# Spreading the preparation of attention groups evenly over the tiles of the group before, with a third PSUM bank for late maxima

## The chip, the cores and the metric

The kernel runs on one core of a Trainium2 chip. The time is device microseconds of one execution. TensorE (PE) multiplies matrices into PSUM, VectorE (DVE) and ScalarE (ACT) read PSUM, GpSimd (POOL) works on SBUF alone, and SyncE (SP) issues most of the DMAs. PSUM has eight banks of 128 x 512 fp32, and the kernel gives each a role.

## The reference, cut to what matters

The model is two layers over 1024 latent tokens with a prefix of 256 context tokens, width 1024, all in fp32. Layer 0 has global grouped attention (A, 8 heads on 2 key heads, with normed and rotated queries and keys) and windowed attention (B, 8 heads on 2 key heads, band of +-128 tokens, the whole context and a learned sink logit). Layer 1 has a convolution module and a neighbourhood attention with 8 heads and a bias table. The part at stake is the softmax of all of these:

```
def gqa_attend(q, k, v, bias=None, sink=None):
    s = jnp.einsum("bqhgd,bkhd->bhgqk", q, k, preferred_element_type=jnp.float32) * ATTN_SCALE
    if bias is not None:
        s = s + bias
    if sink is not None:
        ...
    else:
        p = jax.nn.softmax(s, axis=-1)
    return jnp.einsum("bhgqk,bkhd->bqhgd", p.astype(v.dtype), v)
```

The softmax needs the largest score of each query row. The kernel computes it ahead of the attention itself.

## The kernel before, in words

**Precision.** Every operand is split into a high part (rounded to fp32r) and a low part, so a product is three matmuls (`mm3`, lines 332 to 334), or for scores two (lines 509 and 513) and for the values three (460 to 462). `split` (lines 312 and 315) makes the two parts: a copy on ACT, a subtraction on POOL or DVE.

**Groups and tiles.** Attention runs in groups. In layer 0 a group is one block of 128 queries of four heads that share a key head, so 512 columns; there are four units (key heads, order `ORDER`: two of B, two of A) of ten query blocks each, in the order `QORD`. A group's tiles are blocks of 128 keys: two for a block of context queries, four or five for a block of B, ten for a block of A. In layer 1 a group is one head and one half of the columns, with seven tiles; there are 16. `attn_gen` (line 477) walks through all tiles: score products into one of two banks `st`, exponential on ACT (line 521), `split`, and three tiles later (`look`) the products with the values into the bank `ov` (`flush`). After the last tile of a group DVE turns the sums round, takes the reciprocal and scales the output (lines 470 to 473 and `finish`, 670 to 672).

**Preparation.** What a group needs before its first tile is made by two generators whose steps are handed out between the tiles of earlier groups. `attn_prep` (line 402) loads the queries (layer 0, line 607) or the bias rows (layer 1, line 1279), lets four (layer 1: eight) empty steps pass, then goes through `maxes`: a score product into a bank `mx` (lines 620, 632, 640; layer 1: 1312, 1320), and a reduction on DVE (622, 633, 641; 1314, 1321), with a step after each; then one reduction over the pieces (416 to 426, with the sink where there is one). A preparation has 2 maxima for a context block, 6 for a block of B, 10 for a block of A, 6 for a group of layer 1. `attn_fin` (line 430) lets two empty steps pass, transposes the maxima on PE into another `mx` bank (437), and DVE multiplies them with a mask into the extra rows of `QL` (438). The second score product (513) brings them in, so it must wait for 438.

During group g the steps of `attn_fin` of group g + 1 are handed out first, then those of `attn_prep` of group g + 2. How many come with each tile is a whole number that the kernel works out for each group:

```
g.step = -(-(18 * len(ids) + 4) // len(g.tiles))
```

Half of it (rounded down) comes after the tile's score products, the rest after the flush; at the group's last tile all that is left is handed out. It is 3 for ten tiles, 5 for five, 11 for two, and 4 for the seven of layer 1.

**Fill.** `weave` mixes other work in between the tiles: in layer 0 the projections of the next unit and the output products (lines 332 to 334), in layer 1 its own projections and output products. At the end of a unit a stretch is left without fill.

**Order.** The program text only gives each instruction a priority (its place, shifted for fill by `FL`). A planner simulates the engines and puts on each engine's queue what is ready, the oldest first. Tiles that share a tag share buffers in turn: `mx` has two banks, `tr` has one. `tr` serves the transposition of new queries and keys (line 879), the modulation (184, 189) and the sums of the norms (259).

Of the kernel before, what the change touches and what calls it, by code (L numbers as in the profile page):

```python
# [55 lines left out]
FIN = (2, 2)  # L56
# [20 lines left out]
ORDER = (2, 3, 0, 1)  # L77
# [11 lines left out]
def tile_kernel(ctx: ExitStack, tc: tile.TileContext, a, out):  # L89
# [14 lines left out]
    def bank(tag, name):  # L104
        if tag == "pp" and solo[0]:
            turn[0] += 1
            tag = ("pp", "mx")[turn[0] // 2 % 2]
        return ps.tile([P, 512], F32, tag=tag, name=name, bufs=BUFS[tag])

    uid = [0]  # L110
# [332 lines left out]
    def attn_gen(pool, groups, vshare, look, nexts=None):  # L443
# [4 lines left out]
        cnt = [0]  # L448

        def flush():  # L450
            g, t, ph, pl = pend.pop(0)
# [33 lines left out]
        if layer[0]:  # L485
            groups[0].copy()
        for gi, g in enumerate(groups):
            ids = [gi + 2] if gi + 2 < len(groups) else []
            if nexts is not None and gi in nexts:
                ids = nexts[gi]  # L490
            nx = [preps[k] for k in ids]
            if gi + 1 < len(groups):
                nx.insert(1 if ids[:1] == [gi + 1] else 0, attn_fin(groups[gi + 1]))
            g.next = chain.from_iterable(nx)
            g.step = -(-(18 * len(ids) + 4) // len(g.tiles))
        for g, t in items[:AHEAD]:
            g.ahead(t)
        for x, (g, t) in enumerate(items):
# [26 lines left out]
            if t == len(g.tiles) // 2:  # L525
                g.gate()
            for _ in range(g.step // 2):
                next(g.next, None)
            yield
            if len(pend) > look:  # L530
                flush()
            for _ in range(g.step - g.step // 2):
                next(g.next, None)
            if t == len(g.tiles) - 1:
                for _ in g.next:
                    pass
# [64 lines left out]
    def group0(u, qb):  # L601
        isb = u >= 2
# [11 lines left out]
        def maxes(QH, mp):  # L614
            KA = KAs[u]
            for i2 in range(2):
                mx = bank("mx", nm("mx"))
                for i in range(2):
                    hd = 2 * i2 + i
                    PE.matmul(mx[:, i * 256 : (i + 1) * 256], QH[:, hd * P : (hd + 1) * P], KA[:, 0:256],  # L620
                              start=True, stop=True)
                VE.tensor_reduce(mp[:, 2 * i2 : 2 * i2 + 2, 0], mx.rearrange("p (i k) -> p i k", i=2),
                                 axis=AX.X, op=ALU.max)
                yield
            if qb < 2:
                return
            for hd in range(4):
                q = QH[:, hd * P : (hd + 1) * P]
                if not isb:
                    for k in range(2):  # L630
                        mx = bank("mx", nm("mx"))
                        PE.matmul(mx, q, KA[:, 256 + k * 512 : 768 + k * 512], start=True, stop=True)  # L632
                        VE.tensor_reduce(mp[:, hd, 1 + k : 2 + k], mx, axis=AX.X, op=ALU.max)  # L633
                        yield
                else:
                    lo, hi = max(qb - 1, 2), min(qb + 2, 10)
                    n = (hi - lo) * P
                    mo = (lo - (qb - 1)) * P
                    mx = bank("mx", nm("mx"))
                    PE.matmul(mx[:, :n], q, KA[:, lo * P : hi * P], start=True, stop=True)  # L640
# [25 lines left out]
        def finish(ov, rb):  # L666
# [9 lines left out]
            else:  # L676
# [7 lines left out]
                  tiles=[(k, 0, 512, x) for k, x in kt], den=den, finish=finish)  # L684
        g.prep = attn_prep(kvp, g)
        return g

# [332 lines left out]
    with ExitStack() as l1x:  # L1020
# [241 lines left out]
        def group1(gi, hd, hf):  # L1262
# [41 lines left out]
            def maxes(QH, mp):  # L1304
                KA = Ks[hd % len(Ks)][0]
                for b in (1, 2, 0, 3):
                    if b in (1, 0):
                        mx = bank("mx", nm("mx1"))
                        b0 = 1 - b
# [8 lines left out]
                    n, o = (r1 - r0) * NW, 256 + hf * 640 + r0 * NW  # L1318
                    mx = bank("mx", nm("mx1"))
                    PE.matmul(mx[:, :n], QH[:, b * P : (b + 1) * P], KA[:, o : o + n], start=True, stop=True)  # L1320
# [12 lines left out]
            def finish(ov, rb):  # L1333
# [6 lines left out]
                if i == 3:  # L1340
# [4 lines left out]
                      k=lambda: Ks[hd % len(Ks)], load_v=None, v=lambda k: Vs[gi % 2][:, k if k < 2 else k - 5 * hf, :])  # L1345
            g.prep = attn_prep(kvs[-1], g)
            return g

# [266 lines left out]
```

## Time and profile before

| | |
|---|---|
| median of 3 runs | 1559.18 us (1557.75 to 1565.87) |
| profiled execution | 1559.91 us |
| its span, first to last instruction | 1558.1 us |
| instructions | 21469 |
| mean granted PE clock | 0.965 |
| maxima's products in layer 0 | 160 (line 620), 128 (632), 64 (640) |
| maxima's products in layer 1 | 64 (1312), 64 (1320) |

A row of an engine gives its busy time, a row of waits the engine and line that waited, what it waited for, the sum of the waits in us, their number and the longest. A row of a timeline gives the start and the length in us, the engine, line, operation, tiles and shape, and in brackets how long the engine was idle before. Windowed groups run from about 130 to 489 us, the two units of global attention to about 890, layer 1's attention from about 1205 to 1500.

### The profile page before, as it was taken

The numbers are of one execution on the slowest core, as the hardware profiler recorded it, in microseconds if no ns is written. First come the engines' busy times: TensorE is split into PE (matmuls) and PEld (weight loads), VectorE is DVE, ScalarE is ACT, GpSimd is POOL, SyncE is SP. The second block draws the span as 40 slices with busy tenths as digits, with TensorE's granted clock in tenths as the row PEclk, the third lists the DMA queues.
The fourth block names the chain that finished last, engine by engine and source line by source line (L and its number), as shares of the span: only waits on it lengthen the run. The fifth ranks groups of instructions, "written<-read, shape, count | busy, mean of one in ns | idle before, by whom it ended". The sixth has DMA issues, their size and how long they took to land.

```text
span 1558.1 us, 21469 instructions
## 1 busy us (share of the span) xinstructions
PE 1459.1 (94%) x7084; PEld 1175.6 (75%) x7084; DVE 1050.0 (67%) x2113; ACT 746.9 (48%) x1418; POOL 801.5 (51%) x637
## 2 busy tenths in 40 slices
PE   6899999998998989999999878999999899989995
PEld 2786978896896768876866657888887688868875
DVE  2833557579579765466677846999756566577866
ACT  3721434444435564447556663443334355455563
POOL 3530434455445765557656664665632344364675
PEclk9899999999999999999999889999999899999996
DMA  9473315422312245121112012111445777878632
GB/s 366 161 244 124 108 57 181 143 70 92 119 51 79 92 151 177 54 68 50 51 31 92 7 34 86 58 55 41 142 159 192 216 204 236 263 227 243 183 111 108
DMA packets 154168, 199.83 MB, mean 128 GB/s; under 512 B 14716, under 2 KB 95816, under 8 KB 154056
## 3 DMA queue, kind: packets, MB, share of 16 engines
q1 hardware_dynamic: 147392, 186.88, 38.0%
q10 hardware_dynamic: 6664, 11.57, 2.3%
q8 instruction: 56, 0.92, 0.2%
q14 instruction: 56, 0.46, 0.1%
HBM read 148.07 MB, written 49.02 MB: 126 GB/s over the span
## 4 chain that ended last, share of the span: by engine, by line
PE 79%; DVE 13%; DMA 3%; issue 2%; ACT 2%; POOL 1%; SPq 0%; DVEq 0%; POOLq 0%; ACTq 0%
PE p L332 7%; PE p L333 7%; PE p L334 7%; PE ov L460 4%; PE ov L462 4%; PE ov L461 4%; PE st L509 4%; PE st L513 4%; PE po L333 4%; PE po L332 4%; PE po L334 4%; PE pq L332 3%; PE pq L334 3%; PE pq L333 3%; PE pm L184 2%
## 5 line engine op out<-in xcount | busy, mean ns | idle before, releaser
L315 POOL TENSOR_TENSOR pl<-pf,ph 128x512 fp32r<-128x512 f32 (+4 forms) x321 | 396.8, 1247 | 375.8 <-ACT ph L312 328.7
L521 ACT ACTIVATE pf<-st 128x512 f32<-128x512 f32 x284 | 166.3, 597 | 210.3 <-PE st L513 171.0
L315 POOL TENSOR_TENSOR wl<-wr,wh 128x512 fp32r<-128x512 f32 (+2 forms) x131 | 170.5, 1313 | 141.4 <-ACT wh L312 121.4
L312 ACT CAST ph<-pf 128x512 fp32r<-128x512 f32 (+4 forms) x364 | 209.2, 588 | 29.0 <-PE ov L461 16.7
L332 PE MATMUL p<-hh,wh 128*128 128x512 f32 x448 | 178.2, 398 | 5.3 <-ACT hh L312 2.8
L333 PE MATMUL p<-hl,wh 128*128 128x512 f32 x448 | 176.1, 394 | 0.6 <-POOL hl L315 0.6
L334 PE MATMUL p<-hh,wl 128*128 128x512 f32 x448 | 173.7, 394 | 0.0
L509 PE MATMUL st<-QH,KAt 128*128 128x512 f32 (+4 forms) x364 | 140.9, 388 | 8.9 <-ACT pf L521 8.1
L460 PE MATMUL ov<-ph,Vt 128*128 128x512 f32 (+4 forms) x364 | 142.5, 392 | 5.6 <-DVE y L670 4.3
L462 PE MATMUL ov<-pl,Vt 128*128 128x512 f32 (+4 forms) x364 | 141.9, 390 | 1.8 <-POOL pl L315 1.8
L461 PE MATMUL ov<-ph,Vt 128*64 128x512 f32 (+4 forms) x364 | 140.5, 386 | 0.0
L513 PE MATMUL st<-QL,KBt 68*128 68x512 f32 (+4 forms) x364 | 136.4, 386 | 2.0 <-DVE QL L438 2.0
L1085 DVE SCALAR_TENSOR_TENSOR cps<-U,taps,cps 128x512 f32<-128x512 f32 x184 | 126.4, 751 | 0.9
L312 ACT CAST wh<-wr 128x512 fp32r<-128x512 f32 (+2 forms) x134 | 81.2, 613 | 92.3 <-DMA wr<-in_od_d_dram 19.1
L332 PEld LDWEIGHTS p<-hh,wh 128*128 128x128 f32 x448 | 85.1, 190 | 23.8 <-ACT hh L312 3.0
L333 PEld LDWEIGHTS p<-hl,wh 128*128 128x128 f32 x448 | 85.2, 190 | 18.7 <-POOL hl L315 1.7
L334 PEld LDWEIGHTS p<-hh,wl 128*128 128x128 f32 x448 | 85.1, 190 | 17.5
L633 DVE TENSOR_REDUCE mp<-mx 128x1 f32<-128x512 f32 x128 | 85.2, 681 | 17.4 <-PE mx L632 16.5
L332 PE MATMUL pq<-wh,hh 128*128 128x384 f32 x256 | 88.4, 345 | 2.8 <-ACT hh L312 2.8
L509 PEld LDWEIGHTS st<-QH,KAt 128*128 128x128 f32 x364 | 69.7, 192 | 26.5 <-ACT pf L521 11.9
L954 DVE SCALAR_TENSOR_TENSOR x<-po,modT,x 128x512 f32<-128x512 f32 (+1 forms) x72 | 47.0, 657 | 62.1 <-PE po L334 61.7
L333 PE MATMUL pq<-wl,hh 128*128 128x384 f32 x256 | 87.4, 342 | 0.0
(280 smaller groups left out, 3470.8 us busy)
## 6 DMA issues: line engine op xcount, KB each, us to landing
mw<-in_mod_w_dram SPq DMA_DIRECT2D x16, 1024.0 KB, 5.5
Q<-qs SPq DMA_DIRECT2D x40, 256.0 KB, 2.2
QH<-Q SPq DMA_DIRECT2D x80, 128.0 KB, 2.7
mw<-in_mod_w_dram SPq DMA_DIRECT2D x16, 512.0 KB, 6.7
wr<-in_od_d_dram SPq DMA_DIRECT2D x32, 256.0 KB, 3.2
wr<-in_ev_qkv_dram SPq DMA_DIRECT2D x16, 384.0 KB, 5.2
KAt<-KD SPq DMA_DIRECT2D x16, 384.0 KB, 5.9
wr<-in_od_wo_dram SPq DMA_DIRECT2D x22, 256.0 KB, 3.3
```

The lines of the kernel that those rows point to most:

```text
L312: acts.append(SC.copy(hi, src))
L315: (GP if leng == "g" else VE).tensor_tensor(lo, src, hi.bitcast(F32), op=ALU.subtract)
L332: PE.matmul(o, lh, rh, start=first, stop=False)
L333: PE.matmul(o, lh, rl, start=False, stop=False)
L334: PE.matmul(o, ll, rh, start=False, stop=last)
L460: PE.matmul(o, V[:, 64:192], ph[:, :n], start=(t == 0), stop=False)
L461: PE.matmul(g.ov[0:64, q0 : q0 + n], V[:, 0:64], ph[:, :n], start=False, stop=False)
L462: PE.matmul(o, V[:, 64:192], pl[:, :n], start=False, stop=(last and g.sink is None))
L509: sts.append(PE.matmul(st[:, :n], KA[:, cs], g.QH[:, q0 : q0 + n], start=True, stop=False))
L513: PE.matmul(st[:, :n], KB[0:68, cs], g.QL[0:68, q0 : q0 + n], start=False, stop=True)
L521: acts.append(SC.activation(pf[:, :n], st[:, :n], AF.Exp, scale=1.0 if g.bias else SCALE))
L1085: VE.scalar_tensor_tensor(pc, uc, w, pc, op0=ALU.mult, op1=ALU.add)
```

## The change

A group now carries `units`, the number of steps of its preparation, and `done`, how many steps it has handed out. `advance` hands out steps until `pace` times the number of half tiles so far is reached; `pace` is the number of steps that belong to the group divided by its half tiles, no longer rounded up. In layer 0 a group of two tiles gets a pace of 2.5 a half tile, so ten steps; what is left goes, ahead of its own, to the next group, whose pace counts them in. Everywhere else what is left at the last tile is still handed out there. `mbank` gives every third maximum the bank `tr` in place of `mx`: for all of layer 1, and in layer 0 for the last unit's query blocks from the fourth of `QORD` on. Nothing is added to or taken from the computation.

```
+    third = [0]
+    def mbank(name, wide):
+        third[0] += wide
+        return bank("tr" if wide and third[0] % 3 == 0 else "mx", name)
...
+        def advance(g, n):
+            while g.done < g.pace * n:
+                g.done += 1
+                next(g.next, None)
...
+        rest, over = [], 0
         for gi, g in enumerate(groups):
...
             nx = [preps[k] for k in ids]
             if gi + 1 < len(groups):
                 nx.insert(1 if ids[:1] == [gi + 1] else 0, attn_fin(groups[gi + 1]))
-            g.next = chain.from_iterable(nx)
-            g.step = -(-(18 * len(ids) + 4) // len(g.tiles))
+            units = sum(groups[k].units for k in ids) + FIN[layer[0]] + 1 + over
+            g.spill = not layer[0] and len(g.tiles) == 2 and gi + 1 < len(groups)
+            g.next = chain.from_iterable(rest + nx)
+            rest, over, g.pace = [], 0, units / len(g.tiles) / 2
+            if g.spill:
+                g.pace = 2.5
+                rest, over = [g.next], units - 10
...
-            for _ in range(g.step // 2):
-                next(g.next, None)
+            advance(g, 2 * t + 1)
             yield
             if len(pend) > look:
                 flush()
-            for _ in range(g.step - g.step // 2):
-                next(g.next, None)
-            if t == len(g.tiles) - 1:
+            advance(g, 2 * t + 2)
+            if t == len(g.tiles) - 1 and not g.spill:
                 for _ in g.next:
                     pass
             yield
...
         def maxes(QH, mp):
             KA = KAs[u]
+            wide = u == ORDER[-1] and QORD.index(qb) > 2
             for i2 in range(2):
-                mx = bank("mx", nm("mx"))
+                mx = mbank(nm("mx"), wide)
...
+        g.units, g.done = 4 + 2 + (0 if qb < 2 else 4 if isb else 8) + 1, 0
...
-                        mx = bank("mx", nm("mx1"))
+                        mx = mbank(nm("mx1"), True)
...
+            g.units, g.done = 15, 0
```

More of the change, by code (lines that the diff above doesn't have):

```diff
@@ L630, in maxes @@
                     for k in range(2):
-                        mx = bank("mx", nm("mx"))
+                        mx = mbank(nm("mx"), wide)
                         PE.matmul(mx, q, KA[:, 256 + k * 512 : 768 + k * 512], start=True, stop=True)
@@ L638, in maxes @@
                     mo = (lo - (qb - 1)) * P
-                    mx = bank("mx", nm("mx"))
+                    mx = mbank(nm("mx"), wide)
                     PE.matmul(mx[:, :n], q, KA[:, lo * P : hi * P], start=True, stop=True)
@@ L1318, in maxes @@
                     n, o = (r1 - r0) * NW, 256 + hf * 640 + r0 * NW
-                    mx = bank("mx", nm("mx1"))
+                    mx = mbank(nm("mx1"), True)
                     PE.matmul(mx[:, :n], QH[:, b * P : (b + 1) * P], KA[:, o : o + n], start=True, stop=True)
```

## The prediction

> **What bounds the kernel now.** I read the page's busy table and clock row first, then the chain that ended last, then what TensorE (PE) waited for, then the stretches of the two attention stages, and at the end the instructions around three of the waits.
>
> ```profile
> span 1558.1 us, 21469 instructions
> PE 1459.1 (94%) x7084; PEld 1175.6 (75%) x7084; DVE 1050.0 (67%) x2113; ACT 746.9 (48%) x1418; POOL 801.5 (51%) x637
> PEclk9899999999999999999999889999999899999996
> ...
> PE 79%; DVE 13%; DMA 3%; issue 2%; ACT 2%; POOL 1%; SPq 0%; DVEq 0%; POOLq 0%; ACTq 0%
> ```
>
> PE is the bound: 94% busy, 79% of the chain, and the change adds and removes no instruction. So all that can be won is PE's idle time (1558.1 - 1459.1 = 99.0 us) and the time at a lowered clock. Where that idle time lies is in the next view (columns: stretch, its length, then busy us of each engine, then the granted clock):
>
> ```profile
> 130.00:489.00 359.00, 348.39 (x1827) 291.88 (x1827) 240.86 (x578) 146.48 (x311) 161.99 (x120) 1.00 0.31 101
> 489.00:727.00 238.00, 228.45 (x1081) 181.38 (x1080) 151.94 (x270) 128.20 (x232) 148.34 (x111) 0.99 0.32 101
> 727.00:890.00 163.00, 152.67 (x683) 115.83 (x681) 122.84 (x219) 98.78 (x175) 101.03 (x78) 0.96 0.16 48
> 1205.00:1500.00 295.00, 280.65 (x1392) 231.90 (x1392) 197.71 (x461) 149.58 (x297) 138.84 (x126) 0.96 0.76 222
> ```
>
> The windowed groups (130 to 489), the first global unit (to 727), the last unit (to 890) and layer 1's attention (1205 to 1500) hold 10.6 + 9.6 + 10.3 + 14.3 = 44.8 us of idle PE; the other 54 us lie in the start, the middle and the tail, which the change doesn't touch. In the last unit DVE is busy 122.84 of 163.00 us, its highest share of the four. Of the 44.8 us, these waits of PE belong to the preparation steps (us in total, times, longest):
>
> ```profile
> PE mx L632 <- DVE mp L633: 7.6, 14, 2.1
> PE mx L1320 <- DVE mp L1321: 4.1, 3, 3.4
> PE mx L1312 <- DMA KAt<-KD: 3.5, 1, 3.5
> PE trn L437 <- DVE nmt L426: 2.1, 3, 1.3
> PE mx L620 <- DVE QL L438: 2.1, 3, 1.1
> PE st L513 <- DVE QL L438: 2.0, 1, 2.0
> PE mx L640 <- DVE mp L622: 1.6, 2, 0.9
> PE mx L1320 <- DVE mp L1314: 1.4, 3, 0.8
> PE trn L437 <- DVE nmt L416: 1.0, 1, 1.0
> PE mx L632 <- DVE mp L622: 0.4, 2, 0.2
> ```
>
> Three kinds: a product for a maximum waits until DVE has emptied one of the two banks (layer 0: 7.6 + 1.6 + 0.4 = 9.6; layer 1: 4.1 + 1.4 = 5.5); the transposition of the finished maxima (L437), or the product behind it in the same banks (L620), waits for DVE (2.1 + 1.0 + 2.1 = 5.2); and a maximum of layer 1 came before its keys had landed (3.5).
>
> **A stall costs twice.** These rows are the stretches just behind five such stalls:
>
> ```profile
> 583.42 0.50 PE L632 MATMUL mx<-KAt,QH 128*128 128x512 f32 x1 [2.06 <-DVE mp L633]
> 800.94 0.27 PE L437 MATMUL trn<-ident,nmt 128*4 128x128 f32 x1 [1.04 <-DVE nmt L416]
> 802.60 0.50 PE L620 MATMUL mx<-KAt,QH 128*128 128x256 f32 x2 [1.09 <-DVE QL L438]
> ...
> 523.64:527.05 3.41, 3.33 (x10) 2.67 (x11) 3.41 (x7) 2.42 (x6) 1.45 (x1) 0.50 0.54 181
> 585.08:588.49 3.41, 3.41 (x12) 2.63 (x11) 1.12 (x3) 0.60 (x1) 1.30 (x2) 0.50 1.05 364
> 803.54:806.95 3.41, 3.29 (x9) 2.08 (x8) 2.98 (x6) 2.31 (x5) 1.85 (x2) 0.50 0.05 15
> 1370.15:1373.56 3.41, 3.41 (x12) 2.81 (x11) 1.33 (x5) 1.54 (x4) 2.13 (x3) 0.50 1.10 366
> 1380.39:1383.80 3.41, 3.41 (x9) 2.25 (x9) 3.30 (x9) 0.83 (x3) 3.37 (x3) 0.50 0.83 254
> ```
>
> After 1.04 + 1.09 us of idle PE the granted clock was 0.50 for 3.41 us, so PE did half of what it could: 3.41 / 2 = 1.7 us more. The five stretches together are worth 5 x 1.7 = 8.5 us. The Trainium skill ("TensorE: Matmul & The Clock Gate", the part on what is actually happening) puts the drop to half clock behind a whole idle window of about 3.4 us; here 2.06 us in one piece, or 2.1 us in two, were enough, so I go by the rows. By that rule only the 3.45 us stall at 1379.33 would have a clock price, and my sum below would lose its clock term.
>
> **The change, part by part.** (1) Even spread. A ten-tile group hands out 3 + 4 + 10 + 1 = 18 steps (closing the next group's maxima, four empty ones, ten maxima, one to reduce them). Before, 3 a tile, done in tile 6 of 10; after, 0.9 a half tile, done with the last half tile. The ten maxima then fall on some 11 half tiles in place of 6. Five-tile groups: 14 steps, 5 a tile before (tile 3), 1.4 a half tile after. Layer 1: 18 steps on 7 tiles, 4 a tile before (tile 5), 9/7 a half tile after. What that relieves is read here:
>
> ```profile
> 712.30:727.80 15.50, 14.77 (x65) 10.63 (x64) 9.91 (x20) 12.17 (x21) 12.78 (x11) 1.00 0.18 51
> ...
> 712.30:727.80 15.50, 4.29 (x13) 2.12 (x12) 6.79 (x11) 1.00 0.18 51
> 727.80:743.20 15.40, 4.10 (x12) 2.12 (x12) 6.64 (x11) 1.00 0.33 91
> ...
> L633 DVE TENSOR_REDUCE mp<-mx x128: 636/682/693, 489.9 to 890.8; 128x1 f32<-128x512 f32 x128
> ```
>
> In these two ten-tile groups without any fill (the second and third row count the maxima alone) a tile takes 15.5 / 10 = 1.55 us, and one reduction 0.68. Ten in 3 tiles want 6.8 us of DVE in 4.65 us; ten in 5.5 tiles have 8.5 us. So DVE stops being oversubscribed, and the bank waits of layer 0 should mostly go. I take two thirds of 9.6, that is 6.4 us (bounds: 0 and 9.6). Of layer 1's 5.5 us, 3.39 are one wait in the start-up before the first group (1222.40, below), where the pace doesn't act; of the other 2.1 I take half, 1.05 (0 to 2.1). The key wait of 3.5 us: the first maximum is due in tile 5 and no longer in tile 3, but the trace has it after only two score tiles, so it was drawn ahead of its place; half, 1.75 (0 to 3.5).
>
> ```profile
> 1222.40 0.73 PE L1320 MATMUL mx<-KAt,QH 128*128 128x440 f32 x1 [3.39 <-DVE mp L1321]
> 1379.33 0.48 PE L1312 MATMUL mx<-KAt,QH 128*128 128x256 f32 x2 [3.45 <-DMA KAt<-KD]
> ```
>
> Moved along with the steps: in layer 0 the three query loads at the head of a preparation come half a tile later, and in layer 1 the three bias loads two half tiles later. Both stand on SP's queue behind the same buffers as before, and before the first maximum there are now 4 / 0.9 = 4.4 half tiles (3.4 us) in place of 2.7, and 8 / (9/7) = 6.2 in place of 4; loads that land 2.7 us after issue stay covered. Nothing is added to the queues.
>
> ```profile
> QH<-Q SPq DMA_DIRECT2D x80, 128.0 KB, 2.7
> ```
>
> (2) Two-tile groups. There are eight. They pushed 18 (windowed 14) steps into two tiles; now 10, and 8 (or 4) go into the next group. The idle 1.04 and 1.09 us at 800.94 and 802.60 stand behind such a group. Of the 5.2 us of waits around the transposition I take half, 2.6 (0 to 5.2).
>
> (3) Three banks. The third one is free where it is used: the transposition of new queries and keys that shares it ran last at 548.7, and late maxima begin in the last unit, at 727 and after.
>
> ```profile
> L879 PE MATMUL trk<-ident,pc x120: 270/272/447, 74.5 to 548.7; 128*128 128x128 f32 x120
> ```
>
> It costs nothing itself; its gain is in the terms above. If the bank were taken, each third product would wait one reduction, 0.68 us.
>
> (4) Clock: of five half-clock stretches I let three go, 3 x 1.7 = 5.1 (0 to 8.5).
>
> (5) What is new: a group's last maximum is due in its last half tile, and the transposition for the next group at the first half tile of a two-tile group, where it was due after 3 tiles of slack. Queued behind a late transposition on PE are the next score products and all fill. Price of one late one: 1.04 + 1.09 = 2.13 us. I take three of the eight groups: -6.4 (0 to 8 x (2.13 + 1.7) = 30.6).
>
> Sum: 6.4 + 1.05 + 1.75 + 2.6 + 5.1 - 6.4 = 10.5 us. The profiled execution took 1559.91 us (1.8 around its span), 0.7 over the runs' median of 1559.18; so 1559.9 - 10.5 = 1549.4, told against the median **1549 us**. Ends of the sum: 9.6 + 2.1 + 3.5 + 5.2 + 8.5 = 28.9 better, 1530; 30.6 worse, 1590.
>
> **Rivals.** *Readiness, not pace, sets the order.* The 13 and 12 maxima of the rows above are spread over their whole groups already, though they were handed out within six tiles: the planner puts them where bank, DVE and the transposition before them allow. Then the pace changes little and only the third bank acts, in the last unit: half of the 4.3 us of waits there (2.0 + 0.2 + 1.0 + 1.1) and one clock stretch, 2.2 + 1.7 = 3.9; 1555. Against it: in layer 1 the planner's choice moved a maximum ahead of its place, so place still counts when several are ready.
>
> ```profile
> PE mx L632 <- DVE mp L633: 2.0, 5, 0.7
> PE mx L632 <- DVE mp L622: 0.2, 1, 0.2
> ```
>
> *Late maxima at the two-tile groups: slower.* The maxima of the group after a two-tile one end in the last half tile ahead of it, and from there reduction, transposition and its product with the mask (0.68 + 0.27 + 0.68 us and their signals) must fit in two tiles, 3.1 us where there is no fill. If DVE is behind by more than about 1.5 us there, the next group's second score product stalls PE as at 802.60, with its half clock: 3.8 us each, 30.6 for eight. Less the 6.4 + 1.05 + 1.75 + 2.6 = 11.8 won on waits, it is slower by 18.8: 1578. It decides from four such groups on (15.3 against 11.8). For it: DVE's 75% in the last unit, and the case at 800.94. Against: fill covers six of the eight groups, and the spilled steps ease DVE just there.
>
> *The clock doesn't come back.* If other stalls in the same places keep it down, the 5.1 us go: 1554. For it: in the stretch at 523.64 DVE is busy all of the 3.41 us, so DVE's total work is behind it, which the change doesn't shorten. Against it: at 585.08 DVE is busy 1.12 us, and only its order was late. The Trainium skill's rule named above comes to nearly the same time on another ground, that stalls this short don't lower the clock at all; the five rows speak against it.
>
> **How the numbers follow.** Forecast 0.42, readiness 0.34, late maxima 0.17, clock 0.07. What a measurement of this kernel can tell from no change is about 0.5%, 7.8 us: 1551.4 to 1567.0. Faster: most of the forecast (0.38), 0.06 of the second, 0.01 of the last: 0.45. Same: 0.04 of the forecast, 0.25 and 0.06 of these: 0.35. Slower: the third and 0.03 of the second, 0.20. The likeliest case's own range is 1538 to 1556; the range for 8 in 10 reaches over the second and into the third, 1534 to 1572.
>
> **What would show it.** Right: products for maxima waiting for DVE under 4 us in layer 0 (9.6 now); transposition waits near half of 5.2; at most two of the five half-clock stretches left, and PE busy about the same on a shorter span. The second rival: the two groups at 712 to 743 keep their length and their waits. The third: new waits of L437, L620 or L513 behind L438 just after two-tile groups. It would be wrong altogether if a stall of another kind (DVE's finishing steps, the exponentials) grew by what is won here.

## The result, and the profile after

The changed kernel takes 1564.5 us (median of 22 runs, 1559.59 to 1569.28), the kernel before, run beside it, 1561.57 us (22 runs, 1555.22 to 1566.95). The ratio is 1.0022, 95% interval 1.0011 to 1.0032. So the forecast gain of 10 us did not come; what there is, is a loss of some 3 us, clear of the noise but within the 0.5% that the prediction took for no change.

The profiled execution of the changed kernel took 1562.81 us. From its page of the profile: span, busy times, granted clock and chain.

```profile
span 1561.0 us, 21468 instructions
PE 1462.6 (94%) x7084; PEld 1176.0 (75%) x7084; DVE 1052.0 (67%) x2113; ACT 748.7 (48%) x1418; POOL 801.2 (51%) x637
PEclk7899999999999999999999989999999899989996
...
PE 76%; DVE 14%; DMA 4%; issue 3%; POOL 2%; ACT 2%; SPq 0%; DVEq 0%; POOLq 0%; ACTq 0%
```

PE's idle time is 1561.0 - 1462.6 = 98.4 us, where it was 99.0. PE's busy time grew by 3.5 us with the same 7084 matmuls, and the granted clock was at half for 121.9 us of this execution, before 111.5: that is the clock, not more work. The waits of PE that belong to the preparation (us in total, times, longest; lines 632, 640, 620, 437, 513 of before are 648, 656, 636, 443, 530 now, and 1312 and 1320 are 1329 and 1337):

```profile
PE mx L648 <- DVE mp L649: 9.8, 14, 2.2
PE mx L1337 <- DVE mp L1338: 4.1, 4, 3.2
PE mx L1329 <- issue: 2.6, 1, 2.6
PE trn L443 <- DVE mp L1338: 1.6, 1, 1.6
PE mx L656 <- DVE mp L638: 1.6, 2, 0.9
PE trn L443 <- DVE nmt L432: 1.3, 2, 0.8
PE mx L636 <- DVE QL L444: 1.2, 2, 0.7
PE mx L1337 <- DVE mp L1331: 0.8, 1, 0.8
PE mx L1329 <- DVE mp L1331: 0.6, 1, 0.6
PE st L530 <- DVE QL L444: 0.2, 1, 0.2
PE mx L648 <- DVE mp L638: 0.2, 1, 0.2
```

In layer 0 the products for maxima wait 9.8 + 1.6 + 0.2 = 11.6 us for a bank; it was 9.6, and under 4 was expected. Added up by time from the timelines, those up to 794 us stayed much as they were, 8.1 us before and 7.7 after; behind that, in the last unit's groups from the fourth on, they went from 1.5 to 3.9. The transposition and what stands behind it wait 1.3 + 1.2 = 2.5 us where it was 5.2 (the row of line 530 lies in layer 1). The wait for layer 1's keys went from 3.5 to 2.6: the view says "issue", but the keys' load, issued at 1370.7, landed 8.7 us later, just before the product at 1379.50.

The two ten-tile groups without fill, first with all instructions, then the maxima alone (stretch, length, busy us of each engine, clock):

```profile
712.77:727.95 15.18, 14.42 (x63) 10.40 (x62) 9.76 (x19) 12.03 (x20) 12.59 (x11) 1.00 0.18 52
727.95:743.39 15.44, 14.69 (x64) 10.63 (x63) 10.46 (x21) 11.42 (x20) 10.93 (x9) 1.00 0.31 91
...
712.77:727.95 15.18, 3.99 (x12) 1.80 (x10) 6.55 (x10) 1.00 0.18 52
727.95:743.39 15.44, 4.24 (x12) 2.18 (x12) 6.73 (x11) 1.00 0.31 91
```

They take 15.18 and 15.44 us, before 15.50 and 15.40, with 12 maxima each (13 and 12). The stretches at the places of before's five half-clock ones (the fourth row, at 833.58, has none before), then, from the timeline, three stalls:

```profile
526.38:529.79 3.41, 3.41 (x10) 2.53 (x9) 3.41 (x7) 3.04 (x7) 2.49 (x2) 0.50 0.37 129
586.10:589.51 3.41, 3.41 (x16) 2.73 (x17) 2.48 (x4) 1.26 (x3) 2.98 (x3) 1.00 1.01 350
809.68:816.51 6.83, 6.48 (x18) 4.19 (x18) 6.75 (x16) 1.48 (x4) 0.00 (x0) 0.50 0.00 0
833.58:836.99 3.41, 3.37 (x8) 2.40 (x9) 1.00 (x4) 1.64 (x3) 1.28 (x1) 0.50 0.13 38
1369.47:1376.30 6.83, 6.52 (x21) 4.92 (x21) 4.32 (x11) 4.04 (x10) 3.59 (x3) 0.50 1.04 310
1379.71:1383.12 3.41, 3.41 (x12) 2.94 (x12) 2.37 (x7) 0.10 (x1) 1.72 (x2) 0.50 0.85 247
```

```profile
586.10 0.50 PE L648 MATMUL mx<-KAt,QH 128*128 128x512 f32 x1 [2.22 <-DVE mp L649]
809.40 0.58 PE L648 MATMUL mx<-KAt,QH 128*128 128x512 f32 x1 [2.17 <-DVE mp L649]
833.62 0.77 PE L471 MATMUL ov<-ph,Vt 128*128 128x512 f32 x1 [1.97 <-DVE y L686]
```

Of the five stretches, four are still there, two of them twice as long. At 586 the stall itself is still there, 2.22 us (2.06 before), only the clock did not drop behind it this time. At 833 there is a new one, behind a wait for DVE's scaling of a group's output. The longest one of before's last unit is not among the five; it stands around a wait for an exponential (a stretch and a timeline row of before, then the stretch of the changed kernel):

```profile
858.15:868.39 10.24, 9.80 (x27) 7.47 (x28) 7.77 (x18) 3.86 (x8) 3.54 (x3) 0.50 0.04 13
858.59 0.79 PE L509 MATMUL st<-QH,KAt 128*128 128x512 f32 x1 [3.13 <-ACT pf L521]
...
867.73:871.14 3.41, 3.41 (x10) 2.25 (x9) 2.72 (x6) 2.01 (x5) 2.09 (x2) 0.50 0.13 38
```

So the change moved stalls both ways. At the five places half clock went from 17.1 to 20.5 us; from 100 to 1500 us it went from 64.9 to 68.3, which costs 1.7 us more. The other 3.4 us that this pair of executions differ by in clock lie before 100 us, ahead of all attention.

**Waits and clock apart.** Every execution has its granted clock, so time x (1 - clock) tells how much of it went to the clock (if PE was busy while it was low). As means over executions, the changed kernel lost 62.7 us so (22 runs, clock 0.9600) and the kernel before 56.2 (0.9640; 35 later runs, since the clocks of the 22 beside the change are not on record): +6.5. The time itself grew by 3.5 against these. So apart from the clock the change does win 3.0 us, and the clock takes twice that. In which stage the 6.5 us lie can't be read from one pair of executions; the end of the experiments reads all twenty profiles for it.

### The profile page after: what moved, and what is told of

It reads as the page before. It is cut to its first block, busy times and chain, and to the rows that moved or that the text cites. A ratio compares the mean times of both kernels' runs of the same rounds, so it can differ in the third digit from the quotient of the medians.

```text
span 1561.0 us, 21468 instructions
## 1 busy us (share of the span) xinstructions
PE 1462.6 (94%) x7084; PEld 1176.0 (75%) x7084; DVE 1052.0 (67%) x2113; ACT 748.7 (48%) x1418; POOL 801.2 (51%) x637
## 4 chain that ended last, share of the span: by engine, by line
PE 76%; DVE 14%; DMA 4%; issue 3%; POOL 2%; ACT 2%; SPq 0%; DVEq 0%; POOLq 0%; ACTq 0%
PE p L338 7%; PE p L340 7%; PE p L339 7%; PE ov L471 4%; PE ov L473 4%; PE ov L472 4%; PE st L526 4%; PE st L530 4%; PE po L338 4%; PE po L339 4%; PE po L340 4%; PE pq L338 3%; PE pq L340 3%; PE pq L339 3%; PE pg L338 2%
## 5 line engine op out<-in xcount | busy, mean ns | idle before, releaser
L538 ACT ACTIVATE pf<-st 128x512 f32<-128x512 f32 x284 | 165.8, 596 | 192.1 <-PE st L530 152.0
L321 POOL TENSOR_TENSOR wl<-wr,wh 128x512 fp32r<-128x512 f32 (+2 forms) x131 | 171.0, 1317 | 143.1 <-ACT wh L318 128.2
L473 PEld LDWEIGHTS ov<-pl,Vt 128*128 128x128 f32 x364 | 70.8, 195 | 23.3 <-POOL pl L321 5.1
```

The lines of the kernel that those rows point to most:

```text
L321: (GP if leng == "g" else VE).tensor_tensor(lo, src, hi.bitcast(F32), op=ALU.subtract)
L473: PE.matmul(o, V[:, 64:192], pl[:, :n], start=False, stop=(last and g.sink is None))
L538: acts.append(SC.activation(pf[:, :n], st[:, :n], AF.Exp, scale=1.0 if g.bias else SCALE))
```

## The experiments

Each is the ratio to the kernel before, run beside it, with its 95% interval; then the difference of the mean time in us, the part of it that went to the clock, and the rest. The clock's part is a mean over the whole execution, the start and the tail among it. The clock's spread over a kernel's runs is about 0.0025, some 4 us, and there are 5 to 35 runs, so the standard error of the clock's part is 1.1 to 1.8 us (2.7 in e16), that of the rest 0.7 to 1.4: parts under some 3 us are not told from nothing.

| | ratio | interval | time | clock | rest |
|---|---|---|---|---|---|
| the change | 1.0022 | 1.0011, 1.0032 | +3.5 | +6.5 | -3.0 |
| e1 spread alone | 1.0052 | 1.0031, 1.0072 | +7.1 | +2.3 | +4.8 |
| e2 spread and passing on | 1.0005 | 0.9987, 1.0023 | +0.3 | +0.6 | -0.3 |
| e3 third bank alone | 0.9972 | 0.9957, 0.9986 | -4.2 | -5.8 | +1.6 |
| e4 steps late | 1.0161 | 1.0139, 1.0184 | +24.6 | +15.0 | +9.6 |
| e5 third bank, layer 0 | 1.0008 | 0.9993, 1.0022 | +1.0 | -1.5 | +2.5 |
| e6 third bank, layer 1 | 0.9990 | 0.9978, 1.0002 | -1.7 | -1.7 | 0.0 |
| e7 third bank, whole last unit | 1.0060 | 1.0039, 1.0080 | +8.3 | +0.9 | +7.4 |
| e8 steps early | 1.0031 | 1.0016, 1.0045 | +4.2 | +7.0 | -2.8 |
| e9 changed layer 0 | 1.0005 | 0.9987, 1.0023 | +0.6 | +3.7 | -3.1 |
| e10 changed layer 1 | 1.0004 | 0.9993, 1.0014 | -0.4 | -1.8 | +1.4 |
| e11 less DVE work | 1.0022 | 1.0004, 1.0040 | +3.7 | -1.9 | +5.6 |
| e13 spread, passing on, layer 0 | 1.0003 | 0.9991, 1.0015 | -0.3 | 0.0 | -0.3 |
| e15 the change, two banks in layer 0 | 0.9993 | 0.9980, 1.0006 | -0.9 | +1.6 | -2.5 |
| e16 more DVE work | 1.0100 | 1.0077, 1.0124 | +16.2 | +7.3 | +8.9 |
| e17 as e13, old steps in 2nd unit | 1.0033 | 1.0019, 1.0047 | +4.9 | +7.6 | -2.7 |
| e18 new steps in 2nd unit only | 0.9998 | 0.9981, 1.0014 | +0.2 | +0.5 | -0.3 |
| e19 as e17, bank in layer 1 | 1.0013 | 0.9999, 1.0027 | +2.1 | +6.7 | -4.6 |
| e20 as e13, another bank for `pm` | 0.9959 | 0.9943, 0.9974 | -6.1 | +2.8 | -8.9 |

**The three parts.** e1: the even spread alone. e2: with the passing on. e3: the third bank alone, with the old steps.

```
e1, e2  mbank:   return bank("mx", name)
e1, e3  g.spill = False
e3      g.step and its two loops as before
```

> The even spread alone: two banks for all maxima, and two-tile groups hand out all their steps again. Theory R (the planner puts maxima where bank, DVE and the transposition before them allow; the place in the program counts little): within 0.2% of before, 1558 to 1565 us against 1561.6; the waits of PE for the maxima's banks in the first three units stay at 6 to 8 us, and so does the half-clock stretch behind the wait of about 2 us near 583. Theory P (the spread wins, the third bank loses it again): 1550 to 1556 us, bank waits of layer 0 under 4 us.

> The even spread and the passing on of what two-tile groups leave, still two banks. Theory R: like the even spread alone within 2 us, since the order of the maxima and of the transpositions among themselves is the same in both. Theory P: 1550 to 1556 us. If the spill by itself makes groups behind a two-tile group late, 1564 to 1570 us and waits of PE behind line 444 there.

> The third bank alone, with the old whole-number steps. It is in use in the last unit from its fourth block on and in layer 1, so all before that should run as in the kernel before. Theory R: the whole difference of the changed kernel, +0.2%, comes from here: 1562 to 1567 us, with waits for banks in the last unit of 2 to 4 us still, as DVE and not the bank is what is full there. Theory P: also slower, 1566 to 1570 us, so that the spread's gain makes up for it. A third theory, that the third bank helps as the earlier forecast had it: 1555 to 1559 us.

The spread alone loses 0.5%, slower than either theory of its expectation; with passing on nothing is left of that, though one theory had the two within 2 us; and the third bank alone is 0.3% faster. The new stalls of the spread are late transpositions (and in e1 one product for a maximum, 2.37 us at 362.40); in the timelines of e1 (two rows) and e2 (one):

```profile
389.51 0.38 PE L443 MATMUL trn<-ident,nmt 128*12 128x128 f32 x1 [2.44 <-DVE nmt L432]
810.89 0.27 PE L443 MATMUL trn<-ident,nmt 128*4 128x128 f32 x1 [2.51 <-DVE nmt L422]
```

```profile
800.65 0.38 PE L443 MATMUL trn<-ident,nmt 128*4 128x128 f32 x1 [2.51 <-DVE nmt L422]
```

So the third rival has its mechanism here: one late transposition costs 2.5 us of idle PE with a half-clock stretch of up to 6.83 us behind it. But there are two of them, not eight, and with passing on one. The larger part of e1's loss lies in the windowed units, which take 370.2 us together for 360.8, with 10.2 us at half clock where the kernel before has none.

**Does the place matter at all?** e4 hands all steps out in the last 40% of a group's half tiles, e8 hands them out twice as fast as before; both with two banks and without passing on.

```
e4  while g.done < g.pace * half * max(0, n - half * 6 // 10) / (half - half * 6 // 10):
e8  g.step = 2 * -(-(18 * len(ids) + 4) // len(g.tiles))
```

> The opposite of an even spread: every group hands out none of its steps in the first 60% of its half tiles and all of them, evenly, in the last 40%; two banks, no passing on. Theory R: the first two units (windowed groups, to about 490 us) keep their times within 1 us, as the preparation there is late for other reasons than its place; the last unit and layer 1 move a few us, all in all 1558 to 1570 us. Theory P, by which the place in the program sets when maxima run: 1575 us or more, since ten maxima fall on four tiles.

> Twice as many steps with each tile as before, two banks: the other end of the scale on which the even spread is a move to later. Theory R says that the place in the program can only hold a maximum back, not bring it forward: 1559 to 1563 us, no change within 0.2%. If handing out in bursts is what makes the waits (theory P), 1565 to 1572 us with more than 10 us of waits for banks in layer 0.

Late steps lose 1.6%, as the theory by which the place counts had it. Early ones lose 0.3%, where no change was expected, and that is clock (+7.0, the rest -2.8). How far the maxima themselves move can be read from the programs: for each product of a maximum, behind which score tile the planner put it. Against before, in the four units of layer 0 (72, 72, 104 and 104 products):

```
              products moved      mean shift, tiles (minus: earlier)
the change    10   2  15  90      -0.03  -0.04  -0.01  -0.67
e1             8   8  15  72      -0.01  +0.08  -0.01  +0.84
e4            10   7  45  75      -0.01  +0.07  +0.95  +1.61
e8             7   0   0  32                           +0.23
e7             0   0   4  97                           -2.81
```

In the first three units the change moves 27 of 248 products, and even handing out everything in the last 40% shifts those of the two windowed units by less than a tenth of a tile. The maxima there already ran later than their old place. Only a place later than that moves them (e4, third unit, where the stage grew from 234 to 246 us); an earlier one moves next to none (e8, 39 of 352). That was the second rival's premise, and it holds for the maxima. It does not make the steps free to move: e4's windowed units, expected within 1 us, take 370.5 us for 360.8 with their maxima in place. They have 13.7 us at half clock, where before has none: worth 6.8 of the 9.7 us.

**The third bank by places.** e5: in the last unit alone. e6: in layer 1 alone. e7: in the whole last unit and layer 1. All with the old steps.

```
e5  mbank(nm("mx1"), False)
e6  wide = False
e7  wide = u == ORDER[-1]
```

> The third bank in the last unit of layer 0 alone, old steps, two banks in layer 1. If the 0.28% that the third bank won by itself lies in the last unit, this gives it all: 1556 to 1559 us against 1561.4. If it lies in layer 1's start-up and key waits, this gives nothing: 1560 to 1563 us.

> The third bank in layer 1 alone, old steps everywhere. Since the bank in the last unit alone measured +0.08% and in both -0.28%, its share should be about -0.36%: 1554 to 1558 us against 1561.3. If the two only help together: 1559 to 1562 us.

> The third bank for all blocks of the last unit and for layer 1, old steps. Theory R with the banks as what the maxima wait for: the waits of about 0.4 us each for a bank around 717 and 733, in groups without fill, go, the maxima of the last unit run some three tiles earlier, and the time is 1553 to 1558 us. If DVE and not the bank is what is full: the same waits stay, and 1557 to 1560 us as with the third bank from the fourth block on.

In layer 0 alone it is worth nothing, though it moves 59 products 1.2 tiles forward on average over the unit. Used for that unit's first three groups too (e7) it loses 0.6%, where 0.1 to 0.5% faster was expected, although the maxima come 2.8 tiles sooner: here it was the bank that held them, not their place. Those three groups in e7 (a stretch, then one row of the timeline) and the kernel before:

```profile
728.07:800.28 72.21, 68.30 (x310) 53.22 (x309) 42.57 (x78) 39.88 (x67) 41.68 (x32) 0.98 0.16 46
```

```profile
749.02 0.50 PE L338 MATMUL po<-hh,wh 128*128 128x512 f32 x1 [2.82 <-ACT hh L318]
```

```profile
727.79:794.00 66.21, 65.49 (x309) 51.74 (x308) 42.86 (x80) 39.64 (x67) 41.58 (x32) 1.00 0.18 51
```

The work is nearly the same (six output products more, five maxima fewer), the time 72.21 for 66.21 us: PE idles 3.9 us in place of 0.7, 2.82 of it before an output product, and a half-clock stretch follows at 749.4. Maxima that come sooner are no gain by themselves.

**By layers, and the bank on top of the spread.** e9: the change in layer 0, old steps and third bank in layer 1. e10: the change in layer 1 alone. e13: spread and passing on in layer 0 alone, two banks. e15: the whole change, but two banks in layer 0.

```
e9, e10, e13  advance: old loops for one layer (e9, e13: layer 1; e10: layer 0)
e10, e15      wide = False
e13           mbank: return bank("mx", name)
```

> The changed kernel with the old whole-number steps in layer 1 alone: even spread and passing on in layer 0, third bank in both. The changed kernel is 0.2% over before, the third bank alone 0.3% under it. If the spread's cost with three banks lies in layer 0: 1563 to 1566 us, with the wait of about 2 us near 809 and its half clock still there. If it lies in layer 1 and the tail: 1557 to 1560 us.

> Layer 0 as in the kernel before; in layer 1 the even spread and the third bank. Theory S (the spread gives back in layer 1 what the bank wins there, as the changed kernel against its twin with old steps in layer 1 says, +0.17%): 1557 to 1560 us, 0.1 to 0.2% over the bank in layer 1 alone. If the spread costs nothing in layer 1 when layer 0 runs as before: like the bank in layer 1 alone within 0.1%.

> The even spread and the passing on in layer 0 alone, two banks everywhere, old steps in layer 1. Spread in both layers with two banks was +0.05%. If the spread has a cost in layer 0 whatever the banks, as three banks say (+0.33%): 1564 to 1568 us, and then layer 1's spread would have won 0.3% with two banks. If its cost in layer 0 comes only together with the third bank: 1560 to 1563 us.

> The changed kernel with two banks in layer 0: spread in both layers, passing on, third bank in layer 1 alone. If its loss is the sum of small parts (spread in layer 0 +0.03%, bank in the last unit +0.08%, spread and bank in layer 1 +0.04%): 1561 to 1564 us, about 0.1% over before. If the spread and the third bank of the last unit hurt each other (0.33% between the third banks alone and their twin with the spread in layer 0): 1558 to 1561 us.

e15's interval (0.9980 to 1.0006) lies below the change's (1.0011 to 1.0032): without the third bank in the last unit the loss is gone. It is not that bank alone, since e9 has it on top of the spread too and loses 0.05% (up to 0.23% by its interval). In e15 the last unit has one late transposition, in place of the two stalls of the change at 809.40 and 833.62:

```profile
804.18 0.37 PE L443 MATMUL trn<-ident,nmt 128*4 128x128 f32 x1 [2.52 <-DVE nmt L422]
```

The groups of the last unit from the fourth on take 128.2 us in the change and 129.2 in e9; with the spread and two banks 123.8, 125.2 and 123.5 (e2, e13, e15), before 125.8. Part of that is fill: the change and e9 run 114 output products there, the three others 102, before 108. The whole last unit, with all its fill, takes 194.4 and 195.5 us against 191.2 to 192.7, before 192.1. In layer 1 spread and bank together make attention shorter (309.8 us for 311.6), and the tail behind it longer by as much or more (40.0 for 36.0; the same 40.0 in e10 and e15, 36.6 with the bank alone in e6). The first sums of the norms there start 6.0 us behind the last score product, before 2.9; why was not found.

**DVE's load.** e11 moves the low part of the last unit's outputs from DVE to POOL. e16 does the third unit's 64 large reductions twice, 64 x 0.68 = 43.5 us more of DVE.

```
e11  split(y, oh[c][0]..., oh[c][1]..., "s", "g")
e16  if u == ORDER[2]: VE.tensor_reduce(...)   # the same once more
```

> The kernel before, except that in layer 0's last unit the low part of each finished block is taken by POOL and not by DVE (ten instructions of 0.4 to 1.4 us). Theory D, that DVE is what is full in the last unit and what holds maxima, outputs and sums up there: PE's idle time in 800 to 890 us (9.5 us) falls by 2 to 4 us and the time is 1556 to 1560 us. If POOL becomes late in its place, or the order only moves its stalls: 1560 to 1565 us.

> The kernel before, with each of the third unit's 64 large reductions done twice on DVE, the second time over the first one's result: 64 x 0.68 = 43.5 us more DVE work between 490 and 745 us, each bank held twice as long, nothing else changed. If what the maxima wait for there is DVE's free time and the banks: the unit grows by 10 to 40 us, mostly in the groups without fill at its end, where ten maxima then want 13.6 us of a group's 15.5. If there is slack: under 5 us, and the maxima's waits are no matter of DVE or banks at all.

e16's third unit (a stretch) and, over the whole span, its waits; then the same unit of the kernel before:

```profile
495.22:745.32 250.10, 236.22 (x1067) 182.29 (x1068) 183.69 (x329) 126.78 (x227) 145.31 (x110) 0.96 0.30 95
```

```profile
PE st L509 <- ACT pf L521: 9.9, 13, 2.1
PE mx L632 <- DVE mp L633: 4.8, 10, 0.9
PE mx L632 <- DVE mp L635: 4.7, 6, 1.4
```

```profile
493.76:727.79 234.03, 225.08 (x1066) 179.07 (x1065) 148.29 (x263) 125.56 (x226) 146.38 (x109) 0.99 0.32 101
```

35 us more of DVE in this unit (183.69 against 148.29) make it 16.1 us longer: DVE's time is priced here at nearly half, though PE is the bound. Of the 16.1 us, 4.9 are idle time of PE and 6.8 five half-clock stretches in place of two. Over the whole kernel half of the loss is the clock (+7.3 of +16.2). The edit also holds each bank longer, so it does not tell DVE's load from the bank's time. Taking work from DVE in the last unit did not help (e11): its last four groups take 83.5 us in place of 78.3, and which of POOL's work is late there was not looked into.

**The second windowed unit.** Set side by side, the profiles show where layer 0's spread gives back what it wins. With spread and passing on (the change, e2, e9, e13, e15) the first windowed unit takes 197.3 to 198.8 us, with the old steps (before, e3, e5, e6, e7, e10, e11) 199.5 to 201.0; the third 229.5 to 232.3 against 230.4 to 234.4. But the second takes 163.5 to 167.8 against 161.3 to 163.4. About 1 us of this is fill: the change and e13 run three projection products in the second unit that were in the first. And there a product of the modulation (`pm`, line 190, 184 before), which is fill, takes the bank `tr` after the transposed keys, and waits until DVE has made their low part (`KAt`). The kernel before (timelines of DVE and of PE):

```profile
359.14 0.28 DVE L315 TENSOR_TENSOR KAt<-trk,KAt 64x128 fp32r<-64x128 f32 x1
...
359.53 1.02 PE L184 MATMUL pm<-mw,csil 128*32 128x512 f32 x2 [0.85 <-issue]
```

The changed kernel:

```profile
360.52 0.28 DVE L321 TENSOR_TENSOR KAt<-trk,KAt 64x128 fp32r<-64x128 f32 x1
...
360.91 1.02 PE L190 MATMUL pm<-mw,csil 128*32 128x512 f32 x2 [1.99 <-issue]
361.86 0.38 PE L340 MATMUL pg<-hc,wl 128*128 128x256 f32 x1
```

In both `pm` starts 0.39 us after DVE's instruction began, so that is what it waited for, though the view says "issue" (in e8 it names the releaser: 2.10 us, DVE `KAt`). With 0.85 us no half-clock stretch follows, with 1.99 one does, at 362.54, and in e2, e8, e9, e13 and e15 6.83 us of it. Four runs on that: e17 is e13 with the old steps in this unit alone, e18 the spread and passing on in this unit alone, e19 is e17 with the third bank in layer 1, e20 is e13 with `pm` in a projection bank.

```
e17, e19  g.old = layer[0] or gi // 10 == 1
e18       g.old = layer[0] or gi // 10 != 1
e20       tag = "ov" if solo[0] else "pp"
```

> Layer 0 with even spread and passing on as in the run of both in layer 0 alone, two banks, but the second windowed unit (ten groups, from about 331 us) keeps the old steps; layer 1 as before. Theory of the shared bank: in all eight profiles with changed steps in layer 0 the second windowed unit took 163.5 to 167.8 us, in the seven with the old steps 161.3 to 163.4, and five of the six profiles that spread and pass on, or hand out early, have the modulation's product near 360 us waiting 2.0 to 2.1 us (0.85 with the old steps) with a half-clock stretch behind it. Then this unit goes back to about 161.4 us, the first windowed unit keeps 197 to 199 (200.3), and the time is some 4.3 us under that run's: ratio about 0.9975. Theory of chance (the stretches fall where they fall): no change against that run, ratio 1.000 +- 0.0015, with the lost clock found elsewhere.

> The mirror image: even spread and passing on in the second windowed unit alone, old steps everywhere else, two banks. Theory of the shared bank: the unit takes 165 to 168 us, the modulation's product near 360 us waits about 2.0 us with a half-clock stretch behind it, all other stages as before; ratio about 1.0028. Theory of chance: ratio 1.000 +- 0.0015.

> As the first of these, and in layer 1 every third maximum in the third bank with the old steps there (alone it measured 0.999). If the parts add: ratio about 0.9965. If the first gives nothing: 0.999.

> Even spread and passing on in all of layer 0, two banks, layer 1 as before, and the modulation's product of the fill in one of the two projection banks in place of the bank it shares with the transposition of keys. Theory of the shared bank: its wait of 2.0 us near 360 us goes, no half-clock stretch within 5 us behind it, second windowed unit about 162 to 163 us (165.6), ratio about 0.998. Rival: the projections that share the new bank wait in its place, ratio 1.000 to 1.002.

One row of the timelines of e17, e18 and e20 each:

```profile
359.05 1.34 PE L190 MATMUL pm<-mw,csil 128*32 128x512 f32 x4 [2.25 <-issue]
```

```profile
361.47 1.05 PE L190 MATMUL pm<-mw,csil 128*32 128x512 f32 x4 [1.12 <-issue]
```

```profile
352.54 1.06 PE L190 MATMUL pm<-mw,csil 128*32 128x512 f32 x6
```

Both expectations on the unit's own steps failed. With the old steps in it (e17) the stall stays, 2.25 us, the unit takes 168.3 us and the kernel loses 0.33%; with the new steps in it alone (e18) the wait is 1.12 us, no stretch follows, the unit takes 163.2 us and nothing is lost. So the stall comes with the changed steps of the unit before it: where that unit ends sooner, the fill meets this bank at another moment. All profiles in which `pm` uses this bank fit: where the first unit takes up to 199.0 us the wait is 2.0 to 2.3, from 199.5 to 201.0 it is 0.9 to 1.1, and above that (e1, e4) 0.2. Without this bank (e20) the wait is gone and no stretch follows, the two windowed units together take 358.8 us (363.0 in e13, 360.8 before), and the kernel is 0.41% faster than before, more than expected and the largest gain here. But the stall and its stretch (2.0 + 3.4 us) are not shown to be the gain. From e13 to e20 the clock's part got worse (0.0 to +2.8) and the rest fell from -0.3 to -8.9; and the second unit, expected near 162 us, takes 169.5 while the first takes 189.3, as the fill runs in another order (11 projection products of the first unit run in the second, and a transposition waits 2.3 us there). Whether the same edit is worth as much without the spread was not run. e19 with the bank in layer 1 is 0.2% under e17 (e6: 0.1% under before), within the intervals of both.

**Where the clock goes.** One execution of each of the twenty kernels was profiled. In the two windowed units the nine kernels with the old steps in the first of them (before, e3, e5, e6, e7, e10, e11, e16, e18) have 0 to 3.4 us at half clock. The eleven with other steps there (the change, e1, e2, e4, e8, e9, e13, e15, e17, e19, e20) have 6.8 to 17.1. On average that is 1.3 us lost against 6.7, so a cost of some 5 us appears in a stage where the kernel before had no stretch at all. It is not the whole account: in e2, e13 and e15, which have it too, the mean loss to the clock is only 0 to 1.6 us above before.

## Why the prediction was wrong

1549 was forecast, 1564.5 measured: faster was the likeliest case, and it is 0.2% slower, which the prediction counts as no change.

**The step that failed most is the clock term (4).** Three of five half-clock stretches were to go, 5.1 us won; the runs show 6.5 us lost as a mean. In the profiled pair the five places alone lose 1.7 us more (17.1 to 20.5 us at half clock). The error is to count only the stretches that were there. Every stall near 2 us can bring one, and the change moves stalls: of the five, four stayed, and others stand at 137.3, 362.5 and 833.6, while those around 858 and 1203 shrank or went. Over all profiles the new stretches lie in the windowed units, where the forecast had none to lose. That the stalls there make up the mean's 6.5 us is likely, not shown.

**Part (1), that an even spread relieves DVE,** was wrong in its premise. It took the rows of a whole group (0.68 us a reduction against 1.55 us a tile) for a picture of steps crowded into three tiles. The same rows said that 12 to 13 maxima were spread over the whole group, and the second rival read them so. The orders show it: 27 of 248 products moved in the first three units. Layer-0 bank waits rose from 9.6 to 11.6 us where 6.4 were to be won. The stall at 583.42 came back at 586.10. In layer 1 the term was read wrongly: of the 2.1 us that it took to lie behind the start-up only 0.31 + 0.44 = 0.75 do, and 0.45 + 0.16 = 0.61 are left of them, so 0.1 us was won for a forecast 1.05. The key wait gave 0.9 for a forecast 1.75.

**Part (2)** has the right number and not the right cause: transposition waits in layer 0 went from 5.2 to 2.5 us, 2.7 won for a forecast 2.6. But with the spread and passing on alone (e2) they are 2.5 + 2.3 + 1.8 = 6.6 us:

```profile
PE trn L443 <- DVE nmt L422: 2.5, 1, 2.5
PE trn L443 <- DVE nmt L432: 2.3, 3, 1.3
PE mx L636 <- DVE QL L444: 1.8, 4, 0.6
```

So they fell only with the third bank, and there the stall behind the two-tile group became one of a maximum (809.40). What passing on is worth beside the spread, 0.47% (e1 against e2), lies in the windowed units, 370.2 us together in e1 and 363.0 in e2.

**Part (3)** said that the third bank costs nothing itself. Alone it does not (e5: 1.0008). On top of the spread the last unit is longer with it, 194.4 us for 191.2 in e15, whose whole kernel is 0.29% faster, and two stalls of the change that e15 does not have stand there, at 809.40 for a maximum and at 833.62 for DVE's scaling of an output. e15 has others in their place, of 2.52 and 1.84 us.

**Part (5)** forecast three late transpositions at 2.13 us. e1 has two, at 2.44 and 2.51, e2 and e15 one, the change none in layer 0: the price was close, the number too high, and each has its clock price, which was only counted in the bound.

**Sum.** Without the clock 5.4 us were forecast as won (6.4 + 1.05 + 1.75 + 2.6 - 6.4), and 3.0 were. That these lie close is luck: neither the 6.4 us of relief nor the 6.4 us of late transpositions came. By the means the clock turned the sign: 11.6 of the 14 us between 10.5 won and 3.5 lost.

**The rivals.** *Readiness* had the mechanism: groups and waits at 712 to 743 stayed. Its 1555 did not follow, since the third bank, the part that it let act, is worth nothing in layer 0. *Late maxima* is seen in e1 (+0.52%), at two places, not at the four from which it was to decide, and not in the change. *The clock doesn't come back* was nearest for the reason that decided, but it only took the gain away; it did not have the clock get worse.

**Open.** The third bank alone is 4.2 us faster (e3), while its two places alone give +1.0 and -1.7: the parts do not add, and most of e3's gain is clock (-5.8). Why the two together keep the clock up was not found.

## What to carry to other kernels

Where a planner sets the order, first see whether an operation runs at its place or later: an operation that is late for want of a buffer or of its input is not moved by an earlier place, and giving it another buffer can move the wait to whoever uses that engine next, as here. Count the clock for each stall that a change makes or moves, not only for those that it removes, and compare mean granted clocks over many runs before reading a difference below 0.5% as waits. A stall in one stage can be set by the end of the stage before it, so undo the change in each stage on its own before the cause is put there.

## What the runs showed of the hardware

**How short a stall drops the clock.** Over the twenty profiles, all single idle gaps of PE that begin at full clock after the first 100 us, and how many had a half-clock stretch behind them. Single means at most 0.1 us of other idle time in the 3.41 us before and behind the gap; behind means that the stretch begins during the gap or at most 3.41 us after its end:

```
gap, us     0.3-0.7  0.7-1.0  1.0-1.3  1.3-1.7  1.7-2.2  2.2-3.0  over 3.0
stretches    0/42     0/34     0/18     0/4     19/32    13/15     8/8
```

So in these runs no single gap below 1.7 us dropped the clock, and every one above 3 did. The counts are not independent, since much the same stalls come back in each kernel. Every stretch is a multiple of 3.41 us long, but for the last one, which the end of the execution cuts off. Whether a gap of 2 us brings one differs from profile to profile for the same stall (2.06 us at 583.42 before: yes; 2.22 at 586.10 after: no). The Trainium skill ("TensorE: Matmul & The Clock Gate", what's actually happening) speaks of a whole idle window of about 3.4 us; the 32 drops behind gaps of 1.7 to 3.0 us say that less is enough.

**Run to run.** Executions of one kernel differ by up to 0.6% (1557.49 to 1567.06 us over 35 runs of the kernel before, with a standard deviation of 2.4 us), and time and mean clock go together: over these runs the correlation is -0.69.
